# Sixteen weight groups of a two-layer decoder trunk computed as seven half-size products instead of eight

## The chip, the cores and the metric

The program runs on one core of a Trainium2 chip. The metric is device time in microseconds (us) of one execution, the median of a few runs. In the core, TensorE (PE) multiplies matrices; a matmul streams a moving operand past a 128x128 stationary operand, which a separate load instruction (PEld) puts in place. VectorE (DVE), ScalarE (ACT) and GpSimd (POOL) do elementwise work, each in the order of its own queue. SyncE (SP) and ScalarE issue DMAs.

## The reference, cut to what matters

Two layers, 512 tokens, width 2048, all in float32. Each layer normalises its input, projects it once, runs three mixers on the slices, and projects their concatenation back into the residual stream:

```
h = rmsnorm(x) ; proj = h @ w_in                       # 2048 x 7696
y_conv = (conv3(cv_c * cv_h) + bias) * cv_b * silu(cv_g)           # 512 columns each
y_sb   = stick_breaking(norm(sb_q), norm(sb_k), sb_v) * silu(sb_g) # 8 heads of 128
g      = log_sigmoid(gl_lr @ gla_w_up + gla_b_up) / 16             # gl_lr has 16 columns
y_gla  = rmsnorm(gla(gl_q, gl_k, gl_v, g)) * silu(gl_g)            # 4 heads
x      = x + concat(y_conv, y_sb, y_gla) @ w_out                   # 2048 x 2048
```

## The kernel before, in words

**Float32 by three fp16 products.** Every large product a*b is computed as a_hi*b_hi + a_hi*b_lo + a_lo*b_hi, where hi is the operand scaled by a power of two and rounded to fp16 and lo is what is left over.

**Weight groups.** All weights are taken in 76 groups of 256 columns (38 per layer), listed in `specs` in the order in which TensorE uses them: per layer the linear attention's V (two groups, the second with the 16 low-rank columns), Q, K and two gates; the first convolution's four; for each of four pairs of heads V, gate, Q and K; the second convolution's four (h, c, gate, b); and eight output groups `gi` = 0 to 7 of `w_out`. When group i starts, `weights()` issues the fetch of group i+2 (two tiles `st` of 1 MB, `fetch`) and prepares group i+1 (`load_`): ScalarE squares and sums the staged weights (`wmax`, L319), GpSimd adds the sums over the partitions (L329), VectorE works out the power-of-two scale in small instructions on 128x1 (`wscale`, L330 to L350), ScalarE writes the hi parts `wh` (L392), VectorE the lo parts `wl` (L399).

**Projections.** A group by columns (`project_cols`, L568 to L570) holds a 128x128 block of weights still and streams 512 tokens: 2 column halves x 16 blocks of the inner dimension x 3 = 96 matmuls of 128x512. A group by tokens (`project_toks`, L576 to L578) holds a 128x128 block of the activations still and streams 256 weight columns: 4 token tiles x 16 x 3 = 192 matmuls of 128x256. `project_by_token` (L601) does the same, one token tile after the other, for the first two groups and the last group of a layer. The convolutions go by columns, V, Q, K and the output groups by tokens.

**The mixers' results** are split into the fp16 pair `mh`, `ml` as each comes out (`mixsplit`, L647 and L648), each branch with its own scale, and the output weights are scaled by the ratios of these (`weight_ratio`, L347). Output groups 0 and 1 take the last blocks that become ready (`late`) at their end. `finish` (L1078) adds an output group's result from PSUM to the residual.

**Order.** Apart from the start-up, Tile's scheduler decides the order of the instructions on each engine when the program is built, from the code's order, from `high_priority` blocks and from its own timeline. On the chip each engine follows that order strictly. The attention work (scores, values) and the linear attention are thereby interleaved with the projections on TensorE.

Of the kernel before, what the change touches and what calls it, by code (L numbers as in the profile page):

```python
# [5 lines left out]
F32 = mybir.dt.float32  # L6
# [14 lines left out]
XBITS = 8.0  # L21
RED = bass_isa.ReduceOp

# [7 lines left out]
CHUNKS = ((((3, 0), (2, 512)), (3, 2)), (((0, 0), (1, 128)), (0, 1)))  # L31


@with_exitstack
def hybrid_trunk(ctx, tc, x, norm_g, w_in, conv_w, conv_b, sb_qn_g, sb_kn_g,
# [10 lines left out]
    GX = GW + LR  # L46
    NG = D // GW

    const = ctx.enter_context(tc.tile_pool(name="const", bufs=1))
    stage = ctx.enter_context(tc.tile_pool(name="stage", bufs=3))  # L50
    wpool = ctx.enter_context(tc.tile_pool(name="wpool", bufs=3))
    big = ctx.enter_context(tc.tile_pool(name="big", bufs=4))
# [32 lines left out]
    xs = dram.tile([seq, D], F32, tag="xs", name="xs")  # L85
    xt = [newbig("x", [P, 2, D], F32) for _ in range(2)]
# [22 lines left out]
    parno = wk([P, 32], "raw", 1)  # L109
# [130 lines left out]

    V.tensor_scalar(xsc.bitcast(I32), xun.bitcast(I32), -1.0, float(254 << 23), ALU.mult, ALU.add)
# [30 lines left out]
    specs = []  # L272
    for l in range(depth):
        for cols in ([(GL_V, GW)], [(GL_V + GW, GW), (GL_LR, LR)], [(GL_Q, GW)], [(GL_K, GW)],
                     [(GL_G, GW)], [(GL_G + GW, GW)]):
            specs.append((l, w_in, cols))
        conv = [[(l, w_in, [(c0 + j * GW, GW)]) for c0 in (CV_H, CV_C, CV_G, CV_B)] for j in range(2)]
        specs += conv[0]
        for j in range(4):
            for c0 in (SB_V, SB_G, SB_Q, SB_K):  # L280
                specs.append((l, w_in, [(c0 + j * GW, GW)]))
        specs += conv[1]
        for gi in range(NG):
            specs.append((l, w_out, [(gi * GW, GW)]))
# [10 lines left out]
    def junk(n):  # L295

        return wk([P, HK * GX], "junk", 1, dt=U8)[:, :n]


    def fetch(i):  # L300

        l, src, cols = specs[i]
        staged[i] = st = []
        for h in range(2):
            s_ = stage.tile([P, HK, GX], F32, tag="st", name=nm("st"))
            o = 0
            for c0, w in cols:
                nc.sync.dma_start(
                    s_[:, :, o:o + w],
                    src[l, h * HK * P:(h + 1) * HK * P, c0:c0 + w].rearrange("(k p) n -> p k n", p=P))  # L310
                o += w
            st.append(s_)

    def wmax(i, h):

        n = sum(c[1] for c in specs[i][2])
        if h == 0:
            peak[i] = sm(2, "wm")
        S.activation(junk(HK * n).rearrange("p (k n) -> p k n", k=HK), staged[i][h][:, :, :n], AF.Square,  # L319
                     accum_out=peak[i][:, h:h + 1])  # L320

    def wscale(i):

        l, src, cols = specs[i]

        m = sm(1, "wq")
        if i:
            gm = sm(2, "wgm")
            G.partition_all_reduce(gm, peak.pop(i), P, RED.add)  # L329
            V.tensor_scalar(m, gm[:, 0:1], gm[:, 1:2], 2.0 ** -120, ALU.add, ALU.max)  # L330
        else:

            ps = bank(psm, "m")[:, :1]
            pk = peak.pop(i)
            for j, (a, b) in enumerate(((ones, pk[:, 0:1]), (ones, pk[:, 1:2]), (pk[:, 2:3], pk[:, 2:3]))):
                T.matmul(ps, a.to_broadcast([P, P]), b, start=j == 0, stop=j == 2)
            V.tensor_scalar(m, ps, 2.0 ** -120, None, ALU.max)
        V.tensor_scalar(m.bitcast(I32), m.bitcast(I32), 0x7F000000, None, ALU.bitwise_and)
        sc = sm(1, "ws")
        V.tensor_scalar(sc.bitcast(I32), m.bitcast(I32), -0.5, float(204 << 23), ALU.mult, ALU.add)  # L340
        p2 = sm(1, "wp")
        V.tensor_scalar(p2.bitcast(I32), m.bitcast(I32), 0.5, float(50 << 23), ALU.mult, ALU.add)
        u = sm(1, "wu", bufs=6)
        sw = None
        if src is w_out:
            sw = sm(8, "wsr")
            V.tensor_scalar(sw, ratio[l][0], sc, None, ALU.mult)  # L347
            V.tensor_tensor(u, p2, ratio[l][1], ALU.mult)
        else:
            V.tensor_tensor(u, p2, xun[:, l:l + 1], ALU.mult)  # L350
        loaded[i] = ([], u)
        scales[i] = (sc, sw)

    def wparts(i, h):
        sc, sw = scales[i]
        return [(slice(2 * j, 2 * j + 2), sw[:, h * 4 + j:h * 4 + j + 1]) for j in range(4)] \
            if sw is not None else [(slice(0, HK), sc)]
# [13 lines left out]

    def whi0(h, q, eng):

        if q == 0:
            wh = wpool.tile([P, HK, GX], F16, tag="wh", name=nm("wh"))
            wl = wpool.tile([P, HK, GX], F16, tag="wl", name=nm("wl"))
            loaded[0][0].append((wh, wl))
        wh = loaded[0][0][h][0]
        ks = slice(q * (HK // 2), (q + 1) * (HK // 2))
        if eng is S:  # L380
            S.activation(wh[:, ks, :GW], staged[0][h][:, ks, :GW], AF.Copy, scale=scales[0][0])
        else:
            V.tensor_scalar(wh[:, ks, :GW], staged[0][h][:, ks, :GW], scales[0][0], None, ALU.mult)

    lasthi = {}

    def whi(i, h):
        n = sum(c[1] for c in specs[i][2])
        wh = wpool.tile([P, HK, GX], F16, tag="wh", name=nm("wh"))
        wl = wpool.tile([P, HK, GX], F16, tag="wl", name=nm("wl"))  # L390
        for ks, s_ in wparts(i, h):
            lasthi[i] = S.activation(wh[:, ks, :n], staged[i][h][:, ks, :n], AF.Copy, scale=s_)  # L392
        loaded[i][0].append((wh, wl))

    def wlo(i, h):
        n = sum(c[1] for c in specs[i][2])
        wh, wl = loaded[i][0][h]
        for ks, s_ in wparts(i, h):
            V.scalar_tensor_tensor(wl[:, ks, :n], staged[i][h][:, ks, :n], s_, wh[:, ks, :n],  # L399
                                   ALU.mult, ALU.subtract)  # L400

    def load_(i):

        with tc.issue_after(lasthi[i - 1].ins):
# [3 lines left out]
        for h in range(2):  # L408
            whi(i, h)
            wlo(i, h)  # L410
# [40 lines left out]
    def xhigh(t, h, dst):  # L451
# [7 lines left out]
        S.activation(dst[0][:, t, h * HK:(h + 1) * HK, :], ps, AF.Copy)  # L459

    def xlow(t, h, dst, on_pe):

        ps = xps.pop((t, h))
        xh, xl = (a[:, t, h * HK:(h + 1) * HK, :] for a in dst)
# [7 lines left out]
    def xprep(l, t, dst):  # L472
# [3 lines left out]
        for h in range(2):  # L476
# [6 lines left out]
            parts = wk([P, 2, D // 2], *((("raw", 1), ("qp", 1))[h] if t else ("th", 2)), F16)  # L483
            S.activation(parts[:, 0], xv, AF.Copy)
            V.tensor_tensor(parts[:, 1], xv, parts[:, 0], ALU.subtract)
            for i in range(2):
                nc.sync.dma_start_transpose(dst[i][:, t, h * HK:(h + 1) * HK, :], parts[:, i])  # L487

    def halves(tag):

        return [newbig(tag, [P, NT, KT, P], F16) for _ in range(2)]

    mix = halves("x")
# [26 lines left out]
    wlo(0, 0)  # L520
    wlo(0, 1)
# [21 lines left out]
    whi(1, 0)  # L543
    xlow(3, 0, mix, False)
    xlow(3, 1, mix, False)
    wlo(1, 0)
    whi(1, 1)
    wlo(1, 1)
    make_masks()
    order.__exit__(None, None, None)  # L550

    for l in range(depth):
        last = l == depth - 1
        xh, xl = mix

        def project_cols():

            w, u = weights()
            ps = [bank(psp, "p") for _ in range(2)]
            for h in range(2):  # L560
                wh, wl = w[h]
# [567 lines left out]
```

## Time and profile before

| | |
|---|---|
| median of 3 runs | 1742.44 us (1742.14 to 1742.74) |
| span of the profiled execution | 1740.9 us, 30651 instructions |
| TensorE busy | 1726.8 us (99%), 12846 matmuls and as many weight loads |
| VectorE busy | 1068.9 us (61%), 2015 instructions |
| ScalarE busy | 1090.0 us (63%), 1460 |
| GpSimd busy | 75.1 us (4%), 104 |
| DMA | 204.69 MB, mean 118 GB/s; TensorE's clock granted at full speed in all slices |

The profile gives no other time for the profiled execution than its span; the timed runs lie 1.2 to 1.8 us above it. Matmuls are pipelined, so a row's "mean ns of one" is the time from start to end of one matmul and not the distance to the next; the distance is read from a merged row of the timeline. "Idle before" is the time for which the engine had nothing to do ahead of such an instruction, and the arrow names what ended it.

### The profile page before, as it was taken

The page shows a single profiled execution, that of the slowest core. Times are in us where ns is not written, and L with a number is a line of the kernel's source. Part 1 is how long each engine was busy: PE and PEld are TensorE (multiplying, and loading weights), DVE is VectorE, ACT ScalarE, POOL GpSimd, SP SyncE. Part 2 cuts the span into 40 slices and gives each one's busy share as a digit, 9 for nine tenths or more (in the row PEclk, how much of TensorE's full clock was granted, in tenths as well). Part 3 has the DMA queues.
Part 4 walks back from the last instruction along what each step waited for, and adds up shares of the span by engine and source line. Part 5 has one row for each costly group of instructions (what it writes and reads, how often), then busy time and mean ns, then how long its engine had stood idle before and what let it go on. Part 6 is the DMA issues. An engine that isn't in the chain of part 4 may idle for free.

```text
span 1740.9 us, 30651 instructions
## 1 busy us (share of the span) xinstructions
PE 1726.8 (99%) x12846; PEld 1232.4 (71%) x12846; DVE 1068.9 (61%) x2015; ACT 1090.0 (63%) x1460; POOL 75.1 (4%) x104
## 2 busy tenths in 40 slices
PE   8999999999999999999999999999999999999999
PEld 6744556868787754788885455668686868448888
DVE  7556788657665747433474576976575666673431
ACT  7558577667575867455555684766767667663540
POOL 1000000000000000000010000000000000000000
PEclk9999999999999999999999999999999999999999
DMA  6333313335353545444463333133454444453531
GB/s 222 121 97 97 98 58 113 103 104 131 108 140 110 128 121 128 134 158 146 138 148 105 97 97 97 50 121 110 125 124 109 117 124 126 112 132 113 177 124 40
DMA packets 266121, 204.69 MB, mean 118 GB/s; under 512 B 93106, under 2 KB 265212, under 8 KB 265472
## 3 DMA queue, kind: packets, MB, share of 16 engines
q1 hardware_dynamic: 256976, 193.29, 39.0%
q10 hardware_dynamic: 9008, 9.45, 1.6%
q8 instruction: 100, 1.64, 0.4%
q14 instruction: 37, 0.30, 0.1%
HBM read 173.36 MB, written 8.39 MB: 104 GB/s over the span
## 4 chain that ended last, share of the span: by engine, by line
PE 48%; issue 7%; DVE 1%; DMA 1%; SPq 0%; POOL 0%; ACT 0%; POOLq 0%; DVEq 0%
PE psp L576 8%; PE psp L578 8%; PE psp L577 8%; PE psp L570 6%; PE psp L568 6%; PE psp L569 6%; PE psp L601 3%; PE psz L749 1%; PE psm L988 1%; PE psz L944 1%; PE psz L840 0%; DMA m<-raw 0%; DVE wl L399 0%; SPq L487 0%; DMA xs<-x 0%
## 5 line engine op out<-in xcount | busy, mean ns | idle before, releaser
L577 PE MATMUL psp<-wl,m 128*128 128x256 f16 x1664 | 454.0, 273 | 0.0
L578 PE MATMUL psp<-wh,m 128*128 128x256 f16 x1664 | 453.9, 273 | 0.0
L576 PE MATMUL psp<-wh,m 128*128 128x256 f16 x1664 | 453.8, 273 | 0.0
L399 DVE SCALAR_TENSOR_TENSOR wl<-st,ws,wh 128x2048 f16<-128x2048 f32 (+1 forms) x120 | 282.3, 2353 | 193.1 <-ACT wh L392 179.7
L392 ACT ACTIVATE wh<-st,ws 128x2048 f16<-128x2048 f32 (+1 forms) x118 | 236.3, 2003 | 202.6 <-PE psp L569 100.9
L319 ACT ACTIVATE junk<-st 128x2048 uint8<-128x2048 f32 (+1 forms) x150 | 285.5, 1903 | 7.6 <-DMA st<-in_w_out_dram 4.5
L577 PE MATMUL psp<-wl,x 128*128 128x256 f16 x768 | 209.5, 273 | 0.0
L578 PE MATMUL psp<-wh,x 128*128 128x256 f16 x768 | 209.5, 273 | 0.0
L576 PE MATMUL psp<-wh,x 128*128 128x256 f16 x768 | 209.4, 273 | 0.0
L570 PE MATMUL psp<-m,wl 128*128 128x512 f16 x512 | 194.4, 380 | 0.0
L568 PE MATMUL psp<-x,wh 128*128 128x512 f16 x512 | 194.4, 380 | 0.0
L569 PE MATMUL psp<-x,wh 128*128 128x512 f16 x512 | 194.4, 380 | 0.0
L569 PE MATMUL psp<-m,wh 128*128 128x512 f16 x512 | 194.4, 380 | 0.0
L568 PE MATMUL psp<-m,wh 128*128 128x512 f16 x512 | 194.4, 380 | 0.0
L570 PE MATMUL psp<-x,wl 128*128 128x512 f16 x512 | 194.3, 380 | 0.0
L570 PEld LDWEIGHTS <-wl 128*128 128x128 f16 x1024 | 100.1, 98 | 122.8 <-issue 3.7
L569 PEld LDWEIGHTS <-wh 128*128 128x128 f16 x1024 | 100.1, 98 | 117.5 <-issue 1.1
L568 PEld LDWEIGHTS <-wh 128*128 128x128 f16 x1024 | 100.1, 98 | 115.3 <-issue 0.5
L576 PEld LDWEIGHTS <-m 128*128 128x128 f16 x1664 | 162.7, 98 | 19.9 <-issue 0.7
L578 PEld LDWEIGHTS <-m 128*128 128x128 f16 x1664 | 162.6, 98 | 19.4 <-issue 0.5
L577 PEld LDWEIGHTS <-m 128*128 128x128 f16 x1664 | 162.6, 98 | 18.8
L392 ACT ACTIVATE wh<-st,wsr 128x512 f16<-128x512 f32 x128 | 81.6, 710 | 100.5 <-PE psp L578 74.4
(285 smaller groups left out, 2260.4 us busy)
## 6 DMA issues: line engine op xcount, KB each, us to landing
st<-in_w_in_dram SPq DMA_DIRECT2D x120, 1024.0 KB, 5.3
st<-in_w_out_dram SPq DMA_DIRECT2D x32, 1024.0 KB, 5.5
x<-in_x_dram SPq DMA_DIRECT2D x4, 1024.0 KB
qT<-in_x_dram ACTq DMA_DIRECT2D x8, 512.0 KB, 5.3
qT<-xs ACTq DMA_DIRECT2D x8, 512.0 KB
xs<-x SPq DMA_DIRECT2D x14, 256.0 KB, 4.5
out_dram<-kT SPq DMA_DIRECT2D x14, 256.0 KB, 3.7
th<-za SPq DMA_TRANSPOSE x64, 3.6
```

Of the source, the lines that this page charges most:

```text
L319: S.activation(junk(HK * n).rearrange("p (k n) -> p k n", k=HK), staged[i][h][:, :, :n], AF.Square, accum_out=peak[i][:, h:h + 1])
L392: lasthi[i] = S.activation(wh[:, ks, :n], staged[i][h][:, ks, :n], AF.Copy, scale=s_)
L399: V.scalar_tensor_tensor(wl[:, ks, :n], staged[i][h][:, ks, :n], s_, wh[:, ks, :n], ALU.mult, ALU.subtract)
L568: T.matmul(o, wh[:, kk, cs], xh[:, :, k, :], start=st_, stop=False)
L569: T.matmul(o, wh[:, kk, cs], xl[:, :, k, :], start=False, stop=False)
L570: T.matmul(o, wl[:, kk, cs], xh[:, :, k, :], start=False, stop=en)
L576: T.matmul(o, ah[:, t, k, :], wh[:, kk, :n], start=st_, stop=False, skip_group_check=True)
L577: T.matmul(o, ah[:, t, k, :], wl[:, kk, :n], start=False, stop=False, skip_group_check=True)
L578: T.matmul(o, al[:, t, k, :], wh[:, kk, :n], start=False, stop=en, skip_group_check=True)
L601: T.matmul(o[:, :n], a_[:, t, k, :], w[k // HK][part][:, k % HK, :n], start=i == 0 and k == 0, stop=i == 2 and k == KT - 1)
L749: T.matmul(o, src16[sb][a][:, ss], tgt16[tb][b][:, g0:g1].rearrange("p g h c -> p (g h c)"), start=i == 0, stop=i == 2)
L944: T.matmul(z[:, o:o + (t + 1) * P], qT[:, a_, t, hh, :], kT[:, b_, :t + 1, hh, :], start=i == 0 and o % 512 == 0, stop=False, skip_group_c ...
```

## The change: what it does

**Seven products.** For 16 of the 76 groups (output groups 1 to 6 and the second convolution's h and c, in each layer; table `SEVEN`) the product of a 512x2048 matrix with 2048x256 weights is seen as 2x2 blocks (tokens in halves of 256, the inner dimension in halves of 1024, columns in halves of 128) and computed by Winograd's form of Strassen's scheme: seven block products instead of eight, from sums of blocks on both sides. `right(i)` forms the sums of the weights in place in the staging tiles (four additions of 128x1024 on VectorE) and splits seven blocks into hi and lo (seven instructions of 128x1024 on ScalarE, seven on VectorE). `seven` issues the products: by tokens 7 x 2 x 8 x 3 = 336 matmuls of 128x128, by columns 7 x 8 x 3 = 168 of 128x256, and combines them with eight small instructions (`Raw`, `Residual`) of 128x256.

**Sums of the left side.** `x_sums` forms the sums of the normalised input behind the low-rank gate (eight additions and sixteen splitting instructions of 128x1024, sixteen transposing DMAs). For the output groups the mixers' results now go unsplit to DRAM (`spill`), come back as float32 during the second convolution (`mix_load`), are split with one common scale (`mix_split`, eight pairs of 128x1024), and then summed (`mix_sums`: eight additions, eight pairs of splits).

**Beside it.** The scale of a weight group is computed on GpSimd instead of VectorE (`wscale`), the weights lie in quarter tiles (six buffers of a quarter; a seven-product group takes seven), there are four staging buffers instead of three and two `big` ones instead of four, the 16 low-rank columns are staged apart, the gate takes one instruction less per half, and the stick-breaking weights take two vector instructions less per chunk.

```diff
+SEVEN = {"gla": (), "conv0": (), "sb": (), "conv1": (0,1), "out": (1,2, 3, 4, 5, 6)}
-    stage = ctx.enter_context(tc.tile_pool(name="stage", bufs=3))
-    wpool = ctx.enter_context(tc.tile_pool(name="wpool", bufs=3))
-    big = ctx.enter_context(tc.tile_pool(name="big", bufs=4))
+    stage = ctx.enter_context(tc.tile_pool(name="stage", bufs=4))
+    wpool = ctx.enter_context(tc.tile_pool(name="wpool", bufs=6))
+    big = ctx.enter_context(tc.tile_pool(name="big", bufs=2))
...
     def wscale(i):
...
-            V.tensor_scalar(m, gm[:, 0:1], gm[:, 1:2], 2.0 ** -120, ALU.add, ALU.max)
+            E = G
+            E.tensor_scalar(m, gm[:, 0:1], gm[:, 1:2], 2.0 ** -120, ALU.add, ALU.max)
...
+    def right(i):
+        a, b = (staged[i][0][:, :, c * P:(c + 1) * P] for c in range(2))
+        c, d = (staged[i][1][:, :, c * P:(c + 1) * P] for c in range(2))
+        def part(x):
+            w = wtile(i)
+            hi, lo = (w[:, h, :HK * P].rearrange("p (k n) -> p k n", n=P) for h in range(2))
+            his.setdefault(i, []).append(S.activation(hi, x, AF.Copy, scale=scales[i]))
+            V.scalar_tensor_tensor(lo, x, scales[i], hi, ALU.mult, ALU.subtract)
+        part(a)
+        V.tensor_tensor(b, b, d, ALU.add)
+        V.tensor_tensor(a, a, b, ALU.add)
+        part(a)
+        part(c)
+        V.tensor_tensor(c, c, a, ALU.add)
+        V.tensor_tensor(a, a, d, ALU.subtract)
+        part(a)
+        part(b)
+        part(d)
+        part(c)
...
+    def seven(left, by_cols, evict):
...
+        product(o1, 0, True, False)
+            S.activation(s1, o1[:, :2 * P], AF.Copy, scale=ev.unit)
+        product(o2, 1, True, True)
+            ev.add(u2, o2[:, :2 * P], s1)
+        product(o1, 2, False, True)
+        ev.first(o1[:, :2 * P])
+        product(o3, 3, True, True)
+            ev.sub(vv, o3[:, :2 * P], u2)
+        product(o4, 4, True, False)
+        ev.last4(vv, o4[:, :2 * P])
+        product(o2, 5, True, True)
+        ev.plus(0, 1, o2[:, :2 * P], vv)
+        product(o4, 6, False, True)
+        ev.plus(1, 0, o4[:, :2 * P], u2)
...
-        conv_out(1, conv_in(1, go), go)
+        y = conv_in(1, go)
+        m32 = mix_load()
+        s_ = conv_out(1, y, go)
         while later:
             go()
+        LATE = (10, 11, 2, 3)
+        for k in (0, 4, 6, 8, 12, 14, 10, 2):
+            mix_split(k, s_)
+        if any(modes[cursor[0]:cursor[0] + NG]):
+            sums = mix_sums(s_)
...
         for gi in range(NG):
...
+            if modes[cursor[0]]:
+                seven(quarters(sums), False, lambda u: Residual(gi, u, rt, ot))
```

VectorE in front of the first seven-product output group (`gi` = 1) of the first layer, in the program after. L1069 is `mix_split`, L430 the lo part of a weight block of `gi` = 1 (tiles `w_918`, `w_919`), L753 to L756 the sums of the mixers' results, L1086 the lo parts of these sums.

```order
L430 SCALAR_TENSOR_TENSOR w_918_7856<-st_877_7624,ws_915_7847,w_918_7856 128x1024
L1069 SCALAR_TENSOR_TENSOR act1_183<-m_851_7432,rpm_876_7622,act0_182 128x1024
L754 TENSOR_TENSOR m_850_7431<-m_850_7431 128x4x256
L1086 SCALAR_TENSOR_TENSOR raw_896_7806<-m_851_7432,rpm_876_7622,zw_895_7805 128x1024
L753 TENSOR_TENSOR m_851_7432<-m_850_7431,m_851_7432 128x4x256
L430 SCALAR_TENSOR_TENSOR w_919_7859<-st_878_7626,ws_915_7847,w_919_7859 128x1024
L755 TENSOR_TENSOR m_850_7431<-m_851_7432,m_850_7431 128x4x256
```

The sums are one queue with the last splits and the weights of the same group; the sum that the second product needs (`g_894`) comes last but a few:

```order
L1320 SCALAR_TENSOR_TENSOR kT_907_7832<-psp_925_7877,wu_885_7640,qT_906_7830 128x512
L756 TENSOR_TENSOR m_851_7432<-m_851_7432,m_850_7431 128x4x256
L1086 SCALAR_TENSOR_TENSOR g_894_7800<-m_850_7431,rpm_876_7622,g_893_7799 128x1024 x2
L430 SCALAR_TENSOR_TENSOR w_920_7864<-st_877_7624,ws_915_7847,w_920_7864 128x1024
L430 SCALAR_TENSOR_TENSOR w_921_7867<-st_877_7624,ws_915_7847,w_921_7867 128x1024
L430 SCALAR_TENSOR_TENSOR w_922_7870<-st_878_7626,ws_915_7847,w_922_7870 128x1024
```

Before, VectorE did for an output group this (L330 to L348 the next group's scale, `wl` the lo parts of its weights, L1078 `finish`):

```order
L330 TENSOR_SCALAR wq_1000_8575<-wgm_1001_8576 128x1
L338 TENSOR_SCALAR wq_1000_8575<-wq_1000_8575 128x1
L340 TENSOR_SCALAR ws_1002_8580<-wq_1000_8575 128x1
L342 TENSOR_SCALAR wp_1003_8582<-wq_1000_8575 128x1
L347 TENSOR_SCALAR wsr_1005_8585<-ratio_881_7385,ws_1002_8580 128x8
L348 TENSOR_TENSOR wu_1004_8584<-wp_1003_8582,rgm_879_7380 128x1
L399 SCALAR_TENSOR_TENSOR wl_1007_8589<-st_973_8316,wsr_1005_8585,wh_1006_8588 128x2x256 x4
L399 SCALAR_TENSOR_TENSOR wl_1009_8599<-st_974_8318,wsr_1005_8585,wh_1008_8598 128x2x256 x4
L1078 SCALAR_TENSOR_TENSOR x_901_7557<-psp_1010_8608,wu_982_8334,qT_994_8564 128x2x256
L1078 SCALAR_TENSOR_TENSOR x_902_7558<-psp_1011_8609,wu_982_8334,qT_994_8564 128x2x256
```

Now it does this after the second product of output group 3 (`u2`, L1340), until the lo part of that group's fourth block, `w_973`; `st_961` and `st_962` are the staged weights of group 4, and the added row L433 sums two of their blocks:

```order
L438 TENSOR_TENSOR st_932_8087<-st_932_8087,st_933_8089 128x8x128
L1340 SCALAR_TENSOR_TENSOR u2_1009_9052<-psp_1008_9003,wu_969_8515,s1_1007_9001 128x256
L1360 TENSOR_TENSOR qT_989_8907<-u2_1009_9052,qT_989_8907 128x2x128
L433 TENSOR_TENSOR st_961_8499<-st_961_8499,st_962_8501 128x8x128
L430 SCALAR_TENSOR_TENSOR w_973_8530<-st_932_8087,ws_968_8513,w_973_8530 128x1024
L1348 SCALAR_TENSOR_TENSOR x_901_7823<-psp_1006_8952,wu_969_8515,qT_989_8907 128x2x128
L430 SCALAR_TENSOR_TENSOR w_974_8533<-st_932_8087,ws_968_8513,w_974_8533 128x1024
```

The lo parts of a group's later blocks now stand behind the group's own second eviction.

On GpSimd a group's scale took one instruction before, the all-reduce into `wgm`, shown as ISA with its tiles (`bgm` is that of the attention's bound):

```order
L169 ISA bgm_406_3174<-bm_368_2798 128x1
L329 ISA wgm_416_3194<-wm_412_3188 128x2
L329 ISA wgm_443_3446<-wm_439_3440 128x2
L329 ISA wgm_471_3706<-wm_467_3700 128x2
L329 ISA wgm_496_3988<-wm_492_3982 128x2
L169 ISA bgm_509_4122<-bm_464_3695 128x1
L329 ISA wgm_526_4193<-wm_522_4187 128x2
```

Now there is an instruction without operands (a switch of GpSimd's code library) ahead of the all-reduce and another behind it, and four small ones:

```order
L348 ISA
L348 ISA wgm_306_2325<-wm_302_2319 128x2
L352 ISA
L352 TENSOR_SCALAR wq_305_2324<-wgm_306_2325 128x1
L361 TENSOR_SCALAR wq_305_2324<-wq_305_2324 128x1
L363 TENSOR_SCALAR ws_307_2329<-wq_305_2324 128x1
L365 TENSOR_SCALAR wu_308_2331<-wq_305_2324,xub_155 128x1
```

ScalarE's hi parts of the group wait for this chain instead of for VectorE's.

633 lines of the change are left out of this document (411 added, 222 removed).

## The prediction

> **What bounds the kernel now.** I read the page's busy times first, then the slices, the costliest groups, and the timeline of each engine where the change works.
>
> ```profile
> span 1740.9 us, 30651 instructions
> PE 1726.8 (99%) x12846; PEld 1232.4 (71%) x12846; DVE 1068.9 (61%) x2015; ACT 1090.0 (63%) x1460; POOL 75.1 (4%) x104
> PEclk9999999999999999999999999999999999999999
> ```
>
> TensorE is busy 99% of the span at full clock in every slice. It idles 14 us, so time can only come from fewer or shorter matmuls. Busy is not yet peak, so I look for the distance between matmuls of each width:
>
> ```profile
> 44.43 3.66 PE L601 MATMUL psp<-wh,x 128*128 128x256 f16 x32
> 157.98 1.50 PE L749 MATMUL psz<-m 128*128 128x128 f16 x24
> 72.68 0.38 PE L568 MATMUL psp<-x,wh 128*128 128x512 f16 x1
> 72.90 0.38 PE L569 MATMUL psp<-x,wh 128*128 128x512 f16 x1
> L577 PE MATMUL psp<-wl,m 128*128 128x256 f16 x1664 | 454.0, 273 | 0.0
> L570 PEld LDWEIGHTS <-wl 128*128 128x128 f16 x1024 | 100.1, 98 | 122.8 <-issue 3.7
> ```
>
> A merged row lasts one matmul more than its starts are apart. 256 columns: (3.66 - 0.27)/31 = 0.1092 us. 128 columns: (1.50 - 0.22)/23 = 0.0557, each with its own weight load. 512 columns: about 0.216 (0.22 as printed). Distance is thus proportional to width, with 2 to 3 ns on top, and a weight load of 98 ns does not show even at 56 ns.
>
> Now the stage that the change works on most, the output groups, and the stretch ahead of them:
>
> ```profile
> core 0: us, PE busy (x) PEld busy (x) DVE busy (x) ACT busy (x) POOL busy (x), PEclk, DMA share, GB/s
> 687.00:708.00 21.00, 21.00 (x109) 10.30 (x108) 16.41 (x34) 14.42 (x24) 2.44 (x4) 1.00 0.58 137
> 813.00:834.00 21.00, 21.00 (x195) 18.81 (x193) 7.83 (x16) 11.21 (x22) 0.40 (x1) 1.00 0.47 151
> 811.87 0.75 DVE L1078 SCALAR_TENSOR_TENSOR x<-psp,wu,qT 128x512 f32<-128x512 f32 x1 [1.74 <-PE psp L578]
> 832.83 0.75 DVE L1078 SCALAR_TENSOR_TENSOR x<-psp,wu,qT 128x512 f32<-128x512 f32 x1 [1.75 <-PE psp L578]
> ```
>
> The evictions L1078 of two following groups are 832.83 - 811.87 = 20.96 us apart, which is 192 x 0.1092: TensorE runs at its rate. VectorE is busy 7.83 us of such a group, in the last convolution group before them 16.41 of 21.
>
> **The change part by part: TensorE.** An output group goes from 20.96 us to 336 x 0.0557 = 18.72, a gain of 2.24; twelve give 26.9 us. A convolution group goes from 96 x 0.216 = 20.7 to 168 x 0.1092 = 18.35, a gain of 2.4; four give 9.5. Together 36.4 us, if nothing else is waited for. [...]
>
> **VectorE in an output group.** The costs of its instructions:
>
> ```profile
> L1054 DVE SCALAR_TENSOR_TENSOR qp<-raw,qp 128x1024 f16<-128x1024 f32 x16 | 19.6, 1226 | 18.0 <-ACT qp L1053 18.0
> L1044 DVE TENSOR_TENSOR raw<-raw,qr 128x1024 f32<-128x1024 f32 x8 | 9.8, 1226 | 0.3
> L995 DVE SCALAR_TENSOR_TENSOR e<-psm,vu,g 128x256 f32<-128x256 f32 x32 | 13.9, 476 | 0.0
> L770 DVE TENSOR_TENSOR e<-raw 128x256 f32<-128x256 f32 x24 | 10.1, 422 | 3.1 <-PE psm L679 2.8
> 828.35 2.74 DVE L399 SCALAR_TENSOR_TENSOR wl<-st,wsr,wh 128x512 f16<-128x512 f32 x4 [0.24 <-ACT wh L392]
> ```
>
> Seven lo parts and four additions of 1024: 11 x 1.226 = 13.5. Five evictions from PSUM at 0.476 and three additions at 0.422: 3.6. That is 17.1 us in 18.72, where it was 7.83 in 20.96. VectorE is no longer cover, it is the second bound, and its order decides. The order shows the lo part of a group's fourth block behind the second product's eviction: 0.476 + 0.422 + 1.226 + 1.226 = 3.35, and 0.24 of hand-over, against the third product's 48 x 0.0557 = 2.67 that TensorE can do meanwhile. So TensorE waits 0.9 us. In the order this stands in about four of the six groups of a layer: 2 x 4 x 0.9 = 7 us. Bounds: 0 (17.1 still fits into 18.72) and 12 x 2 = 24 us (a hand-over of 0.24 in each of some eight places a group).
>
> **In front of the first seven-product output group.** VectorE's queue from the first `mix_split` to the sum that the second product needs (`g_894`) holds eight lo parts of the mixers' results, three lo parts and three additions of weights, eight additions and seven lo parts of sums, 29 in all at 1.226 = 35.6, two results of the convolution and two evictions at 0.75, and two small ones at 0.476: 39.5 us. It can begin when the second convolution's gate and the common scale are known. In the window from 687 to 708 above VectorE is 78% busy with this gate and the last scores, so I let it begin 5 us ahead of the end of the last convolution group. Behind that end TensorE has this much to do without the sums:
>
> ```profile
> 688.10 1.81 PE L988 MATMUL psm<-th,v 128*128 128x256 f16 x18
> ```
>
> 18 matmuls of the values (1.6), output group 0 (20.96), and the first and third products (5.3; the built order takes the third ahead of the second): 27.9. The wait is 39.5 - 5 - 27.9 = 6.6 us, and 2.2 more for the second product's eviction, which stands behind another eviction and an addition (0.476 + 1.226 + 0.476). That makes 8.8 per layer, 17.6 us in all. Bounds per layer: 0, if the queue begins 14 us ahead, and 17, if it begins 3 us late. The upper end is also reached from another side: block `w_919` takes the buffer that output group 0 reads to its end, and its hi part stands ahead of six of the sums' on ScalarE; from there on 15 instructions of VectorE (18 us) remain. I stay near the middle, because both ends need the queue to be placed badly or well in both layers.
>
> **What is hidden.** `x_sums` puts 16 x 1.226 = 19.6 us on VectorE behind the low-rank gate, while TensorE does Q, K and the gates:
>
> ```profile
> 940.00:980.00 40.00, 40.00 (x181) 17.49 (x179) 22.82 (x54) 25.43 (x30) 3.59 (x4) 1.00 0.33 106
> 980.00:1020.00 40.00, 40.00 (x205) 18.87 (x204) 22.62 (x42) 29.12 (x38) 0.80 (x2) 1.00 0.33 105
> th<-za SPq DMA_TRANSPOSE x64, 3.6
> st<-in_w_in_dram SPq DMA_DIRECT2D x120, 1024.0 KB, 5.3
> ```
>
> VectorE idles 34 us of these 80, so I cost it at nothing; the sixteen transposes (some 4 us each, as `th`) end long before the second convolution needs them. If the cover were gone it would be 20 us a layer, but the linear attention behind it is interleaved with independent groups. The mixers' results return as 12 transfers of 256 KB during 41 us in which two or three groups' weights come too; at 1 MB in 5.3 us this fits, and SyncE's queue, which they are moved into ahead of the weights of output groups 0 and 1, has that much room. In the convolution groups VectorE's lo parts stand ahead of the group that needs them: nothing.
>
> **The scale on GpSimd.** The chain decides when ScalarE's hi parts begin; in an output group they stand directly behind the squares.
>
> ```profile
> L319 ACT ACTIVATE junk<-st 128x2048 uint8<-128x2048 f32 x146 | 277.4, 1900 | 7.5 <-DMA st<-in_w_out_dram 4.5 <-DMA st<-in_w_in_dram 1.2
> L319 ACT ACTIVATION_READ_ACCUMULATOR junk<-st 128x1 f32 x150 | 28.0, 187 | 0.0
> L1053 ACT ACTIVATE qp<-raw 128x1024 f16<-128x1024 f32 x16 | 16.9, 1057 | 44.0 <-DVE raw L1049 25.8 <-DVE raw L1044 18.1
> L1084 ACT ACTIVATE junk<-x 128x256 uint8<-128x256 f32 x32 | 13.3, 416 | 65.8 <-DVE x L1078 65.0 <-ACT junk L1084 0.3
> 26.75 3.52 POOL L633 MEMSET m<- 128x4096 f16 x1 [24.15 <-PE psz L457]
> 30.40 0.73 POOL L169 PARTITION_ALL_REDUCE kgm<-kg  x2
> 412.60 3.06 POOL L329 PARTITION_ALL_REDUCE wgm<-wm  x1 [21.40 <-ACT junk L319]
> ```
>
> ScalarE per output group: two squares (1.90 + 0.19 each), seven hi parts at 1.057, one copy and four small squares at about 0.6 with their reads: 4.2 + 7.4 + 0.4 + 2.4 = 14.4 us. The chain on GpSimd is the all-reduce (0.37 in that pair) and four instructions on 128x1, bounded by the same 0.37 each, so 1.8. The only library switch of the run before stands between the fill that ends at 30.27 and the all-reduce at 30.40, so it shows 0.13 us; the longest all-reduce, 3.06, is my upper bound for one that has to load something. With 0.13, ScalarE has 14.4 + 2.1 in 18.72: nothing.
>
> **Sum.** 36.4 - 17.6 - 7 = 11.8, taken as 12 us: 1740.9 - 12 = 1729 of span, and as the median stands 1.5 us above this span, 1730.
>
> **The rivals.** (1) Everything hides: the order leaves TensorE busy, 1742 - 36 = 1706. For it speaks that the scheduler moved products past each other; against it the 17.1 of 18.7 us. 0.12. (2) The two gains cancel: 17 us per layer in front of the output groups, 1742 - 36 + 34 + 2 to 7 = 1742 to 1747, in effect the same. 0.12. (3) VectorE bounds the output groups, which ends slower: with 0.24 of hand-over at some 20 instructions a group takes 17.1 + 4.8 = 21.9 us, 0.9 more than before. Then 12 x 0.9 + 17.6 - 9.5 = +19: 1761. It decides from 20.3 us a group on. For it speaks that lo parts have long waited for hi parts (0.24 above); against it that ScalarE is ahead in the order. 0.10. (4) A library switch costs: two at 3.06 - 0.37 = 2.7 put 5.4 us on ScalarE, 14.4 + 1.8 + 5.4 = 21.6 in an output group, 0.6 more than before: 12 x 0.6 + 17.6 - 9.5 = +15, 1757. [...] The one switch seen, at 0.13, speaks against it, but no run here switches to and fro. 0.07. [...] 0.04.
>
> **How the numbers follow.** My forecast (1717 to 1739) has 0.55. A measurement of this kernel tells 0.2%, 3.5 us, from no change. Faster: 0.55 + 0.12 = 0.67; the same 0.12; slower 0.10 + 0.07 + 0.04 = 0.21. The range of 1711 to 1752 leaves out half of (1) below and most of (3) to (5) above, 0.2 in all.
>
> **What would show it.** Matmuls of 128x128 on the new line of `seven`, in merged rows at 56 ns each; idle of TensorE ahead of them put down to VectorE or ScalarE, about 25 us, two thirds of it in two stretches ahead of output group 1; evictions of following output groups 19 to 20 us apart; VectorE over 85% busy there; all-reduces on GpSimd still near 0.4 us, with no gap before the small ones. Wrong would make it a TensorE without such gaps, a distance other than 56 ns, or ScalarE idle for GpSimd.

## The result, and the profile after

The changed kernel takes 1869.17 us (median; 1866.94 to 1871.3), 1.0727 times the time before (interval 1.0712 to 1.0742), 126.7 us slower. The forecast was 1730. Of the page after, its span, busy times and two of its slice rows (tenths, 40 slices):

```profile
span 1865.2 us, 35472 instructions
PE 1733.3 (93%) x14862; PEld 1282.6 (69%) x14862; DVE 1199.9 (64%) x1832; ACT 1153.7 (62%) x1542; POOL 202.5 (11%) x454
PE   7899999999999988878768999999999999987999
PEclk9999999999999999988979999999999999998999
```

TensorE's idle time rose from 14.1 us to 1865.2 - 1733.3 = 131.9. Its busy time rose too, although the products are fewer: 1726.8 - 36.4 = 1690.4 was to be expected, 1733.3 is there. The gaps lie at the start, from the end of the first layer's attention to the second layer's start (slices 15 to 22) and around the second layer's output groups 0 and 1 (slices 36 and 37). The timeline of the changed kernel (start, duration, engine, line; in brackets the idle time and what ended it) shows one such place on three engines, between two output groups:

```profile
814.61 0.41 POOL L348 PARTITION_ALL_REDUCE wgm<-wm  x1 [19.14 <-ACT junk L335]
822.83 0.31 POOL L352 TENSOR_SCALAR wq<-wgm 128x1 f32<-128x1 f32 x1 [7.82 <-issue]
823.73 1.15 ACT L429 ACTIVATE w<-st,ws 128x1024 f16<-128x1024 f32 x1 [9.26 <-POOL ws L363]
824.93 0.26 PE L669 MATMUL psp<-w,act 128*128 128x128 f16 x1 [6.11 <-ACT w L429]
805.26 2.84 PE L669 MATMUL psp<-w,g 128*128 128x128 f16 x48
```

The all-reduce ends at 815.02; the first of the small instructions behind it starts 7.8 us later, in a time in which GpSimd waited for nothing that the profile shows ("issue"): there the program has the instruction without operands, the switch, for which the trace has two instructions of 0.08 us in GpSimd's queue, both at 815.0. The expectations below call this time a code load; the trace shows its length, and not what GpSimd does in it. ScalarE waits for the scale, TensorE for ScalarE. The last row is a whole product: 48 matmuls, (2.84 - 0.22)/47 = 0.0557 us apart, as forecast. Summed over the program (groups by line: busy time, mean ns | idle before and its cause):

```profile
L352 POOL TENSOR_SCALAR wq<-wgm 128x1 f32<-128x1 f32 x75 | 47.7, 636 | 553.5 <-issue 553.3
L348 POOL PARTITION_ALL_REDUCE wgm<-wm x75 | 40.9, 545 | 952.6 <-ACT junk L335 891.8 <-ACT qr L190 27.8 <-ACT xr L190 22.1
```

553.3 us in 73 waits is 7.6 us for each scale. The way back, from the small instructions to the next all-reduce, mostly costs nothing: the switch there comes directly behind the small instructions (at 824.5 here), and all-reduces of the scale start directly behind the squares (`junk`, 891.8 of the 952.6 us). One place in each layer is different. The all-reduce of the mixers' common scale (`rgm`) comes soon behind small instructions and waits 7.51 us in issue (the switch is at 731.4), VectorE waits for it, and with it the splits of the mixers' results (first layer; 7.68 us in the second):

```profile
738.73 0.39 POOL L176 PARTITION_ALL_REDUCE rgm<-pmix  x1 [7.51 <-issue]
739.15 0.16 DVE L1048 TENSOR_REDUCE rgm<-rgm 128x1 f32<-128x8 f32 x1 [8.68 <-POOL rgm L176]
```

The pace of the output groups, by the eviction of the second product (`u2`), output groups 2 and 6 of the first layer, then of the second, and there also the all-reduce of the scale for group 3:

```profile
808.66 0.48 DVE L1340 SCALAR_TENSOR_TENSOR u<-psp,wu,s 128x256 f32<-128x256 f32 x1
915.12 0.48 DVE L1340 SCALAR_TENSOR_TENSOR u<-psp,wu,s 128x256 f32<-128x256 f32 x1
1739.22 1.18 POOL L348 PARTITION_ALL_REDUCE wgm<-wm  x1 [20.72 <-ACT junk L335]
1746.26 0.48 DVE L1340 SCALAR_TENSOR_TENSOR u<-psp,wu,s 128x256 f32<-128x256 f32 x1
1828.25 0.48 DVE L1340 SCALAR_TENSOR_TENSOR u<-psp,wu,s 128x256 f32<-128x256 f32 x1
```

That is 26.6 us a group in the first layer and 20.5 in the second, where 20.96 stood before. The layers differ in the place of the squares. The all-reduce for group 3 starts 6.0 us behind group 2's `u2` in the first layer (814.61 against 808.66), so that the 7.82 us behind it stop TensorE (6.11 us above). In the second it starts 7.0 us ahead of `u2`, and no matmul of that layer's output groups waits for a hi part.

### The profile page after: what moved, and what is told of

Read it like the earlier page. It is cut to its first block, busy times and chain, and to the rows that moved or that the text cites. A ratio compares the mean times of both kernels' runs of the same rounds, so it can differ in the third digit from the quotient of the medians.

```text
span 1865.2 us, 35472 instructions
## 1 busy us (share of the span) xinstructions
PE 1733.3 (93%) x14862; PEld 1282.6 (69%) x14862; DVE 1199.9 (64%) x1832; ACT 1153.7 (62%) x1542; POOL 202.5 (11%) x454
## 4 chain that ended last, share of the span: by engine, by line
PE 60%; DVE 13%; issue 13%; ACT 11%; DMA 2%; POOL 2%; ACTq 0%; POOLq 0%; SPq 0%; DVEq 0%
PE psp L632 8%; PE psp L630 8%; PE psp L631 8%; PE psp L614 8%; PE psp L616 8%; PE psp L615 8%; PE psp L642 4%; ACT junk L335 3%; PE psp L669 3%; DVE w L430 2%; ACT w L429 2%; PE psp L666 2%; ACT w L412 1%; PE psz L932 1%; DVE w L416 1%
## 5 line engine op out<-in xcount | busy, mean ns | idle before, releaser
L630 PE MATMUL psp<-w,act 128*128 128x256 f16 x1664 | 456.1, 274 | 6.4 <-ACT act L1068 6.4
L632 PE MATMUL psp<-w,act 128*128 128x256 f16 x1664 | 456.0, 274 | 2.4 <-DVE act L1069 2.4
L631 PE MATMUL psp<-w,act 128*128 128x256 f16 x1664 | 456.1, 274 | 0.0
L416 DVE SCALAR_TENSOR_TENSOR w<-st,ws,w 128x1024 f16<-128x1024 f32 x240 | 304.9, 1280 | 198.6 <-ACT w L412 198.2
L412 ACT ACTIVATE w<-st,ws 128x1024 f16<-128x1024 f32 x236 | 267.9, 1143 | 228.0 <-PE psp L632 94.5
L614 PE MATMUL psp<-act,w 128*128 128x512 f16 x896 | 342.9, 383 | 0.0
L615 PE MATMUL psp<-act,w 128*128 128x512 f16 x896 | 342.4, 382 | 0.0
L616 PE MATMUL psp<-act,w 128*128 128x512 f16 x896 | 342.4, 382 | 0.0
L335 ACT ACTIVATE junk<-st 128x2048 uint8<-128x2048 f32 x150 | 284.9, 1900 | 6.3 <-DMA st<-in_w_in_dram 5.7
L429 ACT ACTIVATE w<-st,ws 128x1024 f16<-128x1024 f32 x112 | 124.1, 1140 | 133.3 <-POOL ws L363 59.3
L430 DVE SCALAR_TENSOR_TENSOR w<-st,ws,w 128x1024 f16<-128x1024 f32 x112 | 140.6, 1281 | 85.8 <-ACT w L429 85.7
L630 PEld LDWEIGHTS <-act 128*128 128x128 f16 x1664 | 163.6, 98 | 27.0 <-ACT act L1068 6.8
L632 PEld LDWEIGHTS <-act 128*128 128x128 f16 x1664 | 163.5, 98 | 24.7 <-DVE act L1069 4.6
L631 PEld LDWEIGHTS <-act 128*128 128x128 f16 x1664 | 163.7, 98 | 20.6 <-issue 0.5
L642 PE MATMUL psp<-w,act 128*128 128x256 f16 (+1 forms) x1152 | 142.4, 285 | 35.0 <-ACT w L412 12.4
L616 PEld LDWEIGHTS <-w 128*128 128x128 f16 x896 | 88.3, 99 | 106.3 <-issue 4.2
L614 PEld LDWEIGHTS <-w 128*128 128x128 f16 x896 | 88.4, 99 | 105.7 <-issue 5.5
L615 PEld LDWEIGHTS <-w 128*128 128x128 f16 x896 | 88.3, 99 | 105.2 <-issue 6.3
L642 PEld LDWEIGHTS <-act 128*128 128x128 f16 x1152 | 115.7, 101 | 59.1 <-issue 17.8
L669 PE MATMUL psp<-w,act 128*128 128x128 f16 x1728 | 113.7, 231 | 34.8 <-ACT w L429 16.7
L348 POOL PARTITION_ALL_REDUCE wgm<-wm x75 | 40.9, 545 | 952.6 <-ACT junk L335 891.8
L669 PEld LDWEIGHTS <-act 128*128 128x128 f16 x1728 | 109.9, 105 | 37.0 <-issue 28.4
```

Source lines behind the costliest of these rows:

```text
L335: S.activation(junk(HK * GW).rearrange("p (k n) -> p k n", k=HK), staged[i][h], AF.Square, accum_out=peak[i][:, h:h + 1])
L412: his.setdefault(i, []).append(S.activation(quarter(i, q, 0)[:, :, :GW], staged4(i, q), AF.Copy, scale=scales[i]))
L416: V.scalar_tensor_tensor(lo[:, :, :GW], staged4(i, q), scales[i], hi[:, :, :GW], ALU.mult, ALU.subtract)
L430: V.scalar_tensor_tensor(lo, x, scales[i], hi, ALU.mult, ALU.subtract)
L614: T.matmul(o, wh, xh[:, k, :, :], start=st_, stop=False)
L615: T.matmul(o, wh, xl[:, k, :, :], start=False, stop=False)
```

## The experiments

**1. Everything small on VectorE.** GpSimd keeps all-reduces and fills.

```diff
-            E = G
+            E = V
...
-            G.tensor_scalar(nu, u, -1.0, None, ALU.mult)
+            V.tensor_scalar(nu, u, -1.0, None, ALU.mult)
...
```

> The changed kernel with the scale's five small instructions, and the five other small multiplications that it gives to GpSimd, on VectorE: GpSimd keeps the all-reduces and fills, so that it never has to load other code. Theory 1 (GpSimd's code loads, 7.8 us between an all-reduce and the small instruction behind it, and the half clock that follows each long wait of TensorE): most of the 126 us vanish, 1715 to 1745 us, and TensorE's waits for ScalarE's hi parts in the output groups (16.7 us) go. Theory 2 (VectorE's queue in the seven-product groups is the bound; ten more small instructions a group on it do not help): 1850 us or more.

Measured: 1770.23 us, 1.0156 (1.0141 to 1.0171). 98.9 us are gone, far from theory 2, yet 25 us remain above the range of theory 1, and 28 above the time before. So GpSimd's small instructions are the largest part and not the only one. In the profiled executions 78 of the 99 us lie between the first layer's second convolution and the second layer's low-rank matmul (642.9 to 1022.6 us in the changed kernel, 640.0 to 942.1 here). TensorE's waits now (engine, line, cause: us in total, times, longest) are these:

```profile
PE psm L1204 <- DVE v L1234: 11.0, 4, 2.8
PE psp L669 <- ACT s L680: 8.1, 4, 5.6
PE psp L642 <- DVE act L511: 6.1, 2, 4.6
```

**2. No seven products, GpSimd as changed.**

```diff
-SEVEN = {"gla": (), "conv0": (), "sb": (), "conv1": (0,1), "out": (1,2, 3, 4, 5, 6)}
+SEVEN = {"gla": (), "conv0": (), "sb": (), "conv1": (), "out": ()}
```

> The changed kernel with the table SEVEN empty: no group in seven products and no sums, the scale still on GpSimd, everything else of the change in place. Theory 1 (GpSimd's code loads): still slower than before, 1765 to 1810 us, since every group's scale comes 8 us later. Theory 2 (the seven-product groups' VectorE work): 1740 to 1750 us.

Measured: 1799.05 us, 1.0326 (1.0305 to 1.0346), as theory 1 has it. Against run 4, which differs by the small instructions alone, GpSimd costs 34.7 us here and 98.9 with the seven products. In a seven-product group ScalarE has seven hi parts to write behind a late scale; that this makes the whole difference is not shown.

**3. The kernel before, with the scale on GpSimd.**

```diff
-            V.tensor_scalar(m, gm[:, 0:1], gm[:, 1:2], 2.0 ** -120, ALU.add, ALU.max)
+            E = G
+            E.tensor_scalar(m, gm[:, 0:1], gm[:, 1:2], 2.0 ** -120, ALU.add, ALU.max)
...
-            V.tensor_tensor(u, p2, xun[:, l:l + 1], ALU.mult)
+            E.tensor_tensor(u, p2, xun[:, l:l + 1], ALU.mult)
```

The power of two is found by arithmetic instead of a bit mask, in as many instructions.

> The kernel before with nothing changed but the scale of a group computed on GpSimd, in six small instructions behind the all-reduce. Theory 1 (GpSimd's code loads): 1760 to 1800 us, with some 8 us on GpSimd between each all-reduce and the next small instruction. Theory 2: 1742 us within 0.3%, since the group's scale is not needed for another 10 us.

Measured: 2067.21 us, 1.1862 (1.1845 to 1.188). The sign is theory 1's, the size is far beyond both. GpSimd's waits by cause:

```profile
POOL wq L332 <- issue: 572.4, 75, 9.2
ACT wh L395 <- POOL ws L343: 410.2, 57, 14.0
DVE qu L1041 <- POOL wu L353: 127.7, 16, 8.8
```

7.6 us a group again, but here VectorE and ScalarE both stand in their queues for it.

**4. No seven products, everything small on VectorE.**

```diff
-SEVEN = {"gla": (), "conv0": (), "sb": (), "conv1": (0,1), "out": (1,2, 3, 4, 5, 6)}
+SEVEN = {"gla": (), "conv0": (), "sb": (), "conv1": (), "out": ()}
...
-            E = G
+            E = V
...
```

> The changed kernel with the table SEVEN empty and all small instructions on VectorE: what is left of the change is the quarter weight tiles, the four staging buffers, the two big buffers, the mixers' way over DRAM and the cheaper gate. Theory 1: 1735 to 1750 us, these parts cost nothing. Theory 3 (the rearranged buffers cost by themselves, as the start that is 13 us longer suggests): 1755 us or more.

Measured: 1764.35 us, 1.0121 (1.0106 to 1.0136): theory 3's side. 22 us come from the rearrangement without any seven products. One wait repeats four times:

```profile
PE psm L1204 <- DVE v L1234: 10.9, 4, 2.7
478.56 0.22 PE L1165 MATMUL psz<-cmask,identb 128*128 128x128 bf16 x1
481.51 0.37 PE L1204 MATMUL psm<-th,v 128*128 128x256 f16 x1 [2.73 <-DVE v L1234]
481.68 0.63 PE L614 MATMUL psp<-act,w 128*128 128x512 f16 x1
482.11 0.63 PE L615 MATMUL psp<-act,w 128*128 128x512 f16 x1
484.55 0.38 PE L615 MATMUL psp<-act,w 128*128 128x512 f16 x1
484.77 0.38 PE L616 MATMUL psp<-act,w 128*128 128x512 f16 x1
```

One matmul of the attention's values stands alone behind the scores, ahead of the next group's matmuls. TensorE waits 2.73 us for it, and then its matmuls of 512 columns are 0.43 us apart instead of 0.22 until 484.5: half the pace (granted clock 0.51 from 481.5 to 484.5). This goes back to a part of the change that the prediction did not cost: `attend` holds the values of a pair's second head back until the next pair's first scores (`held`).

**5. The attention's order of before**, on run 4.

```diff
-            prior = held.pop() if held else lambda: None
-            if j < 3:
-                held.append(lambda: values(1))
-                later.extend((lambda: scores(0), prior, lambda: scores(1), lambda: values(0)))
-            else:
-                later.extend((lambda: scores(0), lambda: (prior(), scores(1)), lambda: values(0), lambda: values(1)))
+            later.extend((lambda: scores(0), lambda: scores(1), lambda: values(0), lambda: values(1)))
```

> No group in seven products, all small instructions on VectorE, and the order of the attention's steps as before: the values of a pair's second head directly after those of the first, instead of held back until after the next pair's first scores. Theory 3a (the held step: one matmul of the values stands alone behind the scores and waits 2.73 us, four times, each followed by some microseconds at half clock): 1743 to 1748 us, and the four waits gone. Theory 3b (the quarter tiles, two big buffers and the mixers' way over DRAM cost): 1758 us or more.

Measured: 1745.22 us, 1.0018 (1.0008 to 1.0027); the four waits are not in the trace. 19.1 us were the held step: four times 2.73 us of waiting, and 7.0 us of TensorE's busy time (1734.0 to 1727.0) for the slow clock behind it (mean granted clock 0.996 in run 4, 1.000 here). Quarter tiles, buffers and the mixers' way over DRAM cost, less what the cheaper gate gives, the 2.8 us that remain.

**6. All sixteen groups in seven products, small instructions on VectorE, order of before.**

```diff
-            E = G
+            E = V
...
-            prior = held.pop() if held else lambda: None
...
+            later.extend((lambda: scores(0), lambda: scores(1), lambda: values(0), lambda: values(1)))
```

> All sixteen groups in seven products, all small instructions on VectorE, the attention's steps in the order of before. If the costs add: 1770 - 17, so 1751 to 1757 us, with 5 us of waits and half clock ahead of each layer's first seven-product output group still there. If the held step was only where a general lateness of VectorE showed: 1766 us or more, the waits having moved elsewhere.

Measured: 1751.76 us, 1.0053 (1.0038 to 1.0068): the costs add. Ahead of output group 1 in the first layer, then in the second:

```profile
749.88 4.54 PE L669 MATMUL psp<-w,act 128*128 128x128 f16 x48 [5.27 <-ACT s L680]
760.28 4.36 PE L669 MATMUL psp<-w,g 128*128 128x128 f16 x46 [3.08 <-DVE g L1086]
...
1605.85 2.78 PE L669 MATMUL psp<-w,act 128*128 128x128 f16 x47 [1.76 <-ACT s L680]
1609.95 0.23 PE L669 MATMUL psp<-w,g 128*128 128x128 f16 x1 [1.32 <-ACT g L1085]
1611.77 0.23 PE L669 MATMUL psp<-w,zw 128*128 128x128 f16 x1 [1.47 <-DVE kT L1315]
1616.55 3.70 PE L669 MATMUL psp<-w,g 128*128 128x128 f16 x33 [4.55 <-DVE g L1086]
```

8.35 and 9.1 us of waits (8.8 was forecast for each), and a product of 48 matmuls takes 4.54 instead of 2.84 us behind the first of them. The waits of 5.27 and 1.76 us are not for a sum: the third product, built ahead of the second, adds onto the first in PSUM and has to wait until ScalarE has copied that (`s`), and this copy stands in ScalarE's queue behind hi parts that wait for VectorE's sums.

**7. Output group 1 in eight products.**

```diff
-SEVEN = {"gla": (), "conv0": (), "sb": (), "conv1": (0,1), "out": (1,2, 3, 4, 5, 6)}
+SEVEN = {"gla": (), "conv0": (), "sb": (), "conv1": (0,1), "out": (2, 3, 4, 5, 6)}
```

> As the run before, with output group 1 too in eight products, so that the sums have 21 us more to be ready. Theory (the queue of splits and sums ahead of the first seven-product group costs some 12 us a layer with the half clock behind it): 1754 - 24 + 4.5, so 1731 to 1738 us. Rival (VectorE has no room at all in this stage and the wait moves to group 2): 1750 us or more.

Measured: 1739.11 us, 0.9981 (0.9972 to 0.999), 1 us past the range. 12.7 us faster than run 6 while 4.5 us of gain are given up: the queue of splits and sums was worth 17 us, not 24.

**8. And the first layer's second convolution in eight products.**

```diff
-                plan(l, w_in, [(c0 + j * GW, GW)], n in SEVEN["conv1" if j else "conv0"])
+                plan(l, w_in, [(c0 + j * GW, GW)], n in SEVEN["conv1" if j and l else "conv0"])
```

> As the run before, and the second convolution of the first layer in eight products, so that no sums of the input are made in the first layer's start. Theory (these sums stop TensorE at the start for 8 us, against 4.8 that the two groups gain): 3 to 4 us faster than the run before, 1727 to 1735 us, and the waits of 4.3 and 4.6 us near 40 and 54 us gone. Rival (the start is longer for another reason): 4 to 5 us slower than the run before.

Measured: 1730.03 us, 0.9925 (0.9909 to 0.9942): faster than both kernels, by 12.4 us than the one before. 9.1 us against run 7 with 4.8 us of gain given up, so the sums had cost 13.9 us. The start gives 10.9 of these: the first matmuls by columns (L614) begin at 84.60 us in run 7 and at 73.67 here. What gives the other 3 was not traced. In the start the sums had stood in VectorE's queue ahead of the split of the normalised input (L511) for which TensorE waited. The timeline of run 7 (L754 and L771 are sums and their lo parts):

```profile
41.67 1.94 PE L502 MATMUL psz<-ident,x 128*128 128x128 f32 x8 [4.24 <-DVE act L511]
...
51.75 1.21 DVE L754 TENSOR_TENSOR x<-x,x 128x1024 f32<-128x1024 f32 x1
52.88 1.22 DVE L771 TENSOR_TENSOR g<-x,g 128x1024 f16<-128x1024 f32 x1
54.20 2.34 DVE L511 TENSOR_TENSOR act<-psz,act 128x1024 f16<-128x1024 f32 x2
55.47 13.93 PE L642 MATMUL psp<-w,act 128*128 128x256 f16 x98 [3.93 <-DVE act L511]
```

The page of run 8, its groups' pace in the second layer (`u2` of the first and the fifth of five, now L1335) and a small wait that returns with three of the five groups in the first:

```profile
span 1728.2 us, 34111 instructions
PE 1702.8 (99%) x14430; PEld 1247.2 (72%) x14430; DVE 1191.2 (69%) x2120; ACT 1132.6 (66%) x1518; POOL 54.9 (3%) x96
1616.04 0.48 DVE L1335 SCALAR_TENSOR_TENSOR u<-psp,wu,s 128x256 f32<-128x256 f32 x1
1691.25 0.48 DVE L1335 SCALAR_TENSOR_TENSOR u<-psp,wu,s 128x256 f32<-128x256 f32 x1
...
784.48 0.22 PE L669 MATMUL psp<-w,zw 128*128 128x128 f16 x1 [0.70 <-DVE w L430]
823.46 0.22 PE L669 MATMUL psp<-w,zw 128*128 128x128 f16 x1 [0.57 <-DVE w L430]
```

18.8 us a group in the second layer, where 18.72 was worked out, and 19.5 in the first (two groups lie between the two waits).

**9. Run 8 with the scale's four instructions on GpSimd**, the products of its results left on VectorE.

```diff
-            E = V
+            E = G
```

> The run with 1730.0 us (output groups 2 to 6 and the second layer's second convolution in seven products, the attention's steps as before), with the four small instructions of the scale back on GpSimd, so that it loads its other code twice for each group, once in the path of the scale. Theory 1 (the load on the path, 7 to 9 us for each group): 1775 to 1830 us, the loss in the first layer's output groups. Rival (the 99 us that GpSimd cost in the changed kernel came from its meeting with the held values and the late sums): 1735 to 1750 us.

Measured: 1981.29 us, 1.1381 (1.1351 to 1.1411): 251 us, far over the expectation. VectorE's waits:

```profile
DVE qu L1252 <- POOL wu L365: 159.8, 16, 17.7
DVE nu L806 <- POOL wu L365: 119.9, 16, 11.3
DVE nu L1347 <- POOL wu L365: 82.7, 10, 9.8
```

Small instructions on VectorE read the late result, and its whole queue stands behind them.

**10. Run 8 with one copy on GpSimd in the path.**

```diff
+            gc = sm(2, "wgc")
+            G.tensor_scalar(gc, gm[:, 0:2], 1.0, None, ALU.mult)
-            E.tensor_scalar(m, gm[:, 0:1], gm[:, 1:2], 2.0 ** -120, ALU.add, ALU.max)
+            E.tensor_scalar(m, gc[:, 0:1], gc[:, 1:2], 2.0 ** -120, ALU.add, ALU.max)
```

> The run with 1730.0 us, with one instruction added: GpSimd copies the all-reduce's 128x2 result, and VectorE works the scale out from the copy. It has one small GpSimd instruction on the path instead of four, and the same two code loads. Theory 1 (the load is the price): within 12 us of the run with all four on GpSimd. Rival (the small instructions themselves and their hand-overs are slow on GpSimd): 1731 to 1738 us, a quarter of the loss or less.

Measured: 2107.79 us, 1.2085 (1.2053 to 1.2118). The rival falls: one instruction on the path costs more than four. VectorE waits for each copy:

```profile
DVE wq L354 <- POOL wgc L353: 662.4, 75, 16.5
```

8.8 us a group, in a queue that every other step needs. That it is 126.5 us above run 9, and not within 12, was not foreseen: there VectorE waited 53 times for `wu`, 438.8 us in all (the rows above and four smaller rows), here for all 75.

**11. The same copy, read by nothing.**

```diff
+            gc = sm(2, "wgc")
+            G.tensor_scalar(gc, gm[:, 0:2], 1.0, None, ALU.mult)
```

> The same copy on GpSimd, but nothing reads it: VectorE works from the all-reduce's result, as in the run with 1730.0 us. GpSimd loads its code as often. Theory 1: 1727 to 1736 us, with 7 to 9 us ahead of each copy, since GpSimd is idle most of the time and loads the other code again before the next group's sums arrive. Rival (loading code disturbs the core's memory traffic or delays the next all-reduce): 1740 us or more.

Measured: 1759.82 us, 1.0098 (1.0083 to 1.0113). Taking the result off the path gives back 348 of 378 us; the expectation of no cost fails by 24 us at its upper end.

```profile
L353 POOL TENSOR_SCALAR wgc<-wgm 128x2 f32<-128x2 f32 x75 | 39.9, 532 | 543.6 <-issue 189.1 <-DVE w L418 105.9 <-DVE qp L1270 63.3
L348 POOL PARTITION_ALL_REDUCE wgm<-wm x75 | 38.4, 512 | 1013.9 <-ACT junk L335 936.8 <-issue 30.6 <-ACT qr L190 15.1
```

The time ahead of a copy is the same, whatever name the profile puts to its end: 7.3 us on average where it says "issue" (189.1 in 26 waits), 7.1 where it says VectorE's L418 (105.9 in 15), 543.6 us or 7.2 a copy in all. The way back comes into the path where the next squares are early: the all-reduces of the scale wait 30.6 us in issue, in four waits, and those of the common scale 14.0 in two. That these make up the 29.8 us lost against run 8 is likely but not shown.

**12. Run 8 with every small instruction on GpSimd as the change has it.**

```diff
-            E = V
+            E = G
-            V.tensor_scalar(nu, u, -1.0, None, ALU.mult)
+            G.tensor_scalar(nu, u, -1.0, None, ALU.mult)
...
```

> The run with 1730.0 us, with every small instruction that the change gives to GpSimd back on GpSimd: the four of the scale and the products of its results (nu, vu, qu, uu). Theory 1a (a code load costs by who stands behind it: with only the scale there, VectorE's queue waited 363 us for GpSimd's result; now no instruction of VectorE reads it early): 1760 to 1810 us, far below 1981. Theory 1b (the held values are what protected the changed kernel from the late scales; here they are not held): 1900 us or more.

Measured: 1833.01 us, 1.0521 (1.0503 to 1.0538), 23 us above 1a's range and 148 below run 9, with 73 waits of 7.3 us on GpSimd:

```profile
L352 POOL TENSOR_SCALAR wq<-wgm 128x1 f32<-128x1 f32 x75 | 55.7, 743 | 534.9 <-issue 534.7
```

1b falls: without the held values the small instructions on GpSimd cost 103.0 us, with them 98.9. That VectorE reads next to nothing of GpSimd's early (three waits of 19.1 us for `wu` in the changed kernel) is what kept that kernel from run 9's loss.

## Why the prediction was wrong, point by point

The difference of 126.7 us in one account, all from medians and rounded: -36.4 for the fewer matmuls (worked out), +98.9 for the small instructions on GpSimd (run 1), +18.5 for the held step (run 1 to 6; 19.1 from run 4 to 5), +2.8 for the rest of the rearrangement (run 5), +17.1 for the queue ahead of output group 1 (run 7), +13.9 for the input's sums (run 8), and +12.0 that run 8 still lacks against run 5: 27.2 were to be gained by its ten output groups and two convolution groups, 15.2 were. In the profiles these 12 are 8.8 us more of TensorE's idle time and 3 us of busy time; the wait that grew most is one for a transposing DMA at the second layer's start, 3.42 us where run 5 has 1.78, and the rest was not traced. The clock counts within these terms.

- **TensorE's gain: right.** 56 ns between matmuls held for whole products with a weight load each (48 in 2.84 us, 0.0557 apart). No run shows weight loads that limit such products, to which the prediction gave 0.04. With the covers mended an output group takes 18.8 us (run 8, second layer).
- **"With 0.13, ScalarE has 14.4 + 2.1 in 18.72: nothing": this step failed.** The scale on GpSimd was put at 1.8 to 2.1 us and is about 9 (ScalarE waits 9.26 for it in the rows above, which is the prediction's own sign of being wrong). The one switch in the trace before was taken as the price of a switch. It stood between a fill and an all-reduce, and such a pair shows no idle time elsewhere either: before, an all-reduce starts at 893.32 us, when a fill ends. The upper bound (3.06, an all-reduce) was the duration of something else. The time ahead of the mixers' common scale, 7.6 us a layer, was not in the sum at all. Rival 4 had the term with 2.7 us a switch and 0.07 of chance; the trace has 7.6.
- **"VectorE idles 34 us of these 80, so I cost it at nothing": failed for one layer.** The windows were those of the second layer. In the first the sums stand in the start, where VectorE is the engine waited for: 10.9 us there, 13.9 in all.
- **The attention's order: left out.** The diff had the line; I costed no moved step there. 18.5 us from one matmul that stands alone, four times.
- **In front of output group 1: right in size, in part by luck** (8.8 forecast, 8.35 and 9.1 in run 6). VectorE's queue of sums is what TensorE waits for in the end, as forecast. But the third product was counted as work that TensorE has meanwhile, and it waited itself, 5.27 us in the first layer, for ScalarE's copy of the first product. What was not counted at all is the clock behind the waits (mean granted clock 0.991 in run 6, 0.996 in run 7): with it the queue cost 17.1 us in run 7's comparison, close to the 17.6 of the sum but made up differently.
- **The waits within output groups:** 0.9 us in four of six was forecast. In run 8 three of the first layer's five groups wait 0.57 to 0.70 us for VectorE's lo part, and their pace is 0.8 above 18.72: mechanism and size fit. The second layer has two such waits, 0.69 and 0.56, for evictions.
- **The clock: not foreseen at all.** Busy time was 42.9 us over 1690.4 in the changed kernel (mean granted clock 0.968), 15.8 in run 1 (0.991), and 3.2 over 1699.6 in run 8 (0.998).

## What to carry to other kernels

A cost seen once in a trace is the price of that occurrence; where a step runs 75 times under other circumstances, keep the bound open, and do not move small work onto an engine that shows such a time between two kinds of its instructions (7.6 us here, from an all-reduce to a small one) before you know which queue will wait for it. The price of a late result is set by the queue that stands behind it: the same 7 to 7.6 us a group cost 35 (run 2), 99 (the changed kernel), 251 (run 9) and 325 us (run 3). When an engine is 99% busy, hold every reordered step against the wait that it can start, and look up the cover in each layer, the start above all.

## What the runs showed of the hardware

Waits of TensorE can cost twice. In the changed kernel, at the start of output group 0, matmuls of 256 columns stand 0.21 us apart behind a wait of 3.42 us (granted clock 0.50), and 0.11 from 747.5 on (1.00):

```profile
740.81 0.40 PE L630 MATMUL psp<-w,act 128*128 128x256 f16 x1 [3.42 <-ACT act L1068]
744.17 0.42 PE L630 MATMUL psp<-w,act 128*128 128x256 f16 x1
744.38 0.42 PE L631 MATMUL psp<-w,act 128*128 128x256 f16 x1
747.87 0.27 PE L631 MATMUL psp<-w,act 128*128 128x256 f16 x1
747.98 0.27 PE L632 MATMUL psp<-w,act 128*128 128x256 f16 x1
```

In run 4 a wait of 2.73 us was enough (matmuls of 512 columns 0.43 us apart behind it), and in the changed kernel one of 2.34 us (at 1723.97; granted clock 0.50 from 1724.0 to 1727.0), while one of 2.74 us in the same kernel was not (at 493.16; 1.00 from 493.2 to 496.5, and 0.22 us apart). So the length of a wait does not decide it alone.
